# The second mixer's input projection in seven-product units entered by token halves, its results kept in DRAM, and squares of second halves added on GpSimd

## The chip, the cores and the metric

The kernel runs on one core of a Trainium2 chip. The metric is device time in microseconds of one launch, as the median of several runs. The profile shows one execution on that core. Engines are named as the profile names them: PE is TensorE (PEld its weight loads), DVE is VectorE, ACT is ScalarE, POOL is GpSimd, SP is SyncE, which here only issues DMAs.

## The reference

Two layers over 1024 tokens of width 1024, float32. Layer 0 has a mixer of gated blocks and forgetting attention, layer 1 a mixer of pooling and short convolution; after each come cross-attention into 256 memory tokens and a SwiGLU feed-forward of width 2816.

```python
for layer in range(2):
    h = rms_norm(x, g_mix[layer])
    y = even_mixer(h, ...) if layer % 2 == 0 else odd_mixer(h, ...)
    x = x + y
    x = x + memory_cross_attention(rms_norm(x, g_xa[layer]), rms_norm(mem, g_mem[layer]), ...)
    h = rms_norm(x, g_ffn[layer])
    x = x + (silu(h @ w_gate[layer]) * (h @ w_up[layer])) @ w_down[layer]

def odd_mixer(h, w_in, w_pool, s_pool, conv_w, w_out):     # w_in: 1024 x 2048
    z = h @ w_in
    zc, hd, gb, gc = z[:, :512], z[:, 512:1024], z[:, 1024:1536], z[:, 1536:]
    # pooling: 4 groups of 128, trailing mean over 2, 4, 8, 16 tokens minus the token,
    # then a 128 x 128 map per group and a scale per channel
    y_c = multiscale_pool(zc, w_pool, s_pool)
    # convolution: three taps over tokens on gc * hd, gated by gb
    y_d = short_gated_conv(hd, gb, gc, conv_w)
    return concat(y_c, y_d) @ w_out                          # w_out: 1024 x 1024
```

## The kernel before

**Number format.** Every float32 operand of a product is split in two: a high part, rounded by an ACT cast, and a low part, the remainder, from a DVE subtraction (`low`, line 551). A product of two such operands takes three matmuls: high x high, high x low, low x high. Data is held transposed: channels on the 128 partitions, tokens along the free dimension. A matmul is 128x128 by 128x512.

**Memory.** Two arenas in SBUF are handed out by a planner in Python as the program is built: `arena_r` (`self.R`, 35840 columns, for the split operands) and `arena_f` (`self.F`, 16384 columns, for plain float32). Each has a region "a" and a region "b". PSUM has eight banks of 512 columns.

**Order.** The program is a list of tasks (`self.add`), each with the operands that it needs. `run` walks the list. Before each task it prepares operands ahead, in order of first use: at most `la` columns ahead, at most `parts_max` columns of weight parts, and at most `raws` raw weights loaded and not yet consumed (`fetch_ahead`); an operand whose task has come must be made at once. `defer` puts off a step by a number of tasks. Each engine executes its instructions in the order in which they were emitted.

**Dense products.** `dense` (used by the second mixer) runs over row blocks of 128 and both halves of 512 tokens, three matmuls each. The normalised input h is not scaled by the token's norm; results are multiplied afterwards by `rbc`, the norm spread over all partitions.

**Seven-product units.** The feed-forward's projections use `Unit` and `seven`: two row blocks and two column blocks of the weight, and the two token halves, form 2x2 blocks, whose product is made with seven block products in place of eight (`Unit.make` forms the weight sums, lines 247 to 256; `Pair.make` those of a pair of input row blocks, lines 330 to 350). A unit over n pairs takes 7 x n x 3 matmuls. `collected` sums PSUM into two tiles of 128x1024 (lines 1973 to 1983) and hands on each quarter as it is finished; `onto_x` (line 2004) adds into x. In the gate and up projections POOL multiplies each gate quarter (line 2026) and makes sums of the products to be stored (line 2058).

**Entry into the feed-forward.** `cross` finishes x by token halves, first all row blocks of half 0, then of half 1. For each, `x_final` writes the half to DRAM (`xs`), scales half 0 in place and sums the squares: for half 0 on POOL (line 1909), for half 1 with four one-column matmuls per row block. `half_stats` then forms the tokens' norms; it and `spread`, which makes `rbc`, come after the first two products of the gate and of the up unit.

**Down projection.** The products of gate and up are stored in DRAM (`pq`) as the seven operands of each of 11 pairs. `VISITS` lists visits (column pair mp, first pair, last pair): each is one unit over some pairs, and a pair's operands stay in `arena_r` from its first to its last visit. The weights are loaded by POOL's queue. The last visits finish x.

**Second mixer.** At the end of the first feed-forward `chunk_sq` sums squares over whole rows (ACT, POOL lines 802 and 803) and `chunk_h` makes h and its low part for whole rows (lines 790, 791) in region "a" of `arena_r`, once `open_now` has taken it. `odd` then makes 16 blocks of z (`z_of`), each scaled by `rbc` (line 2213): four pooled groups (`pool_means`, lines 2225 to 2234; `pool_map`, lines 2250 and 2251) and twelve for the convolution (lines 2261 to 2273). x stays in `arena_f`, the split results in `arena_r`. The output projection comes in two halves (`out_half`, sums at line 1645): pooled results after the first two convolution blocks, convolution results at the end.

## Time and profile before

| | |
|---|---|
| median of 3 runs | 2389.23 us (2389.03 to 2389.98) |
| profiled execution | 2389.92 us, span 2388.1 us |
| mean granted TensorE clock | 0.994 |
| busy PE / DVE / ACT / POOL | 98% / 71% / 43% / 31% |
| first feed-forward, gate and up | from about 660 to 1080 us |
| its down projection | to about 1325 us |
| second mixer | about 1329 to 1595 us |
| second cross-attention, feed-forward | to the end |

In the profile a group's row gives the line, engine, operation, tiles with shapes, and count, then busy time and mean duration in ns, then the engine's idle time just before these instructions and what ended it. A line of the timeline gives start, length (us), engine, line, operation and how many were merged; brackets hold the idle time before. A line that belongs to a helper (551, 256, 539) serves many callers.

### The profile page before, as it was taken

The page shows a single profiled execution, that of the slowest core. Times are in us where ns is not written, and L with a number is a line of the kernel's source. Part 1 is how long each engine was busy: PE and PEld are TensorE (multiplying, and loading weights), DVE is VectorE, ACT ScalarE, POOL GpSimd, SP SyncE. Part 2 cuts the span into 40 slices and gives each one's busy share as a digit, 9 for nine tenths or more (in the row PEclk, how much of TensorE's full clock was granted, in tenths as well). Part 3 has the DMA queues.
Part 4 walks back from the last instruction along what each step waited for, and adds up shares of the span by engine and source line. Part 5 has one row for each costly group of instructions (what it writes and reads, how often), then busy time and mean ns, then how long its engine had stood idle before and what let it go on. Part 6 is the DMA issues. An engine that isn't in the chain of part 4 may idle for free. (4 is left out here: it accounts for less than half of the span.)

```text
span 2388.1 us, 31149 instructions
## 1 busy us (share of the span) xinstructions
PE 2337.4 (98%) x11358; PEld 1976.5 (83%) x11358; DVE 1705.6 (71%) x2505; ACT 1024.2 (43%) x1866; POOL 743.0 (31%) x745
## 2 busy tenths in 40 slices
PE   7999999999999999999999899999999999999999
PEld 7999879988888878887888788888877887877887
DVE  5456457864898888978677553356879988887666
ACT  6346356755554444445224221146544444444221
POOL 6542333343333343433011310033333334342000
PEclk9999999999999999999999999999999999999999
DMA  7336325431224444438873121021233444357783
GB/s 235 119 133 214 97 81 151 125 124 45 89 70 160 142 149 139 153 131 295 279 267 117 50 65 44 28 79 45 89 101 138 150 141 168 118 194 260 254 289 92
DMA packets 227074, 335.57 MB, mean 141 GB/s; under 512 B 12864, under 2 KB 128664, under 8 KB 226920
## 3 DMA queue, kind: packets, MB, share of 16 engines
q1 hardware_dynamic: 214544, 289.32, 37.1%
q0 software_dynamic: 12192, 44.21, 5.2%
q8 instruction: 89, 1.46, 0.3%
q14 instruction: 65, 0.53, 0.1%
q10 hardware_dynamic: 184, 0.05, 0.0%
HBM read 226.44 MB, written 107.09 MB: 140 GB/s over the span
## 5 line engine op out<-in xcount | busy, mean ns | idle before, releaser
L539 PE MATMUL psum_t<-arena_r 128*128 128x512 f32 (+4 forms) x10304 | 2255.4, 378 | 34.2 <-DVE arena_r L551 10.7
L539 PEld LDWEIGHTS psum_t<-arena_r 128*128 128x128 f32 (+1 forms) x10304 | 1856.2, 189 | 380.1 <-DVE arena_r L551 18.3
L551 DVE TENSOR_TENSOR arena_r<-arena_f,arena_r 128x512 fp32r<-128x512 f32 (+4 forms) x803 | 672.1, 857 | 167.5 <-PE psum_t L539 53.2
L256 ACT CAST arena_r<-arena_f 128x512 fp32r<-128x512 f32 (+2 forms) x504 | 282.4, 584 | 429.4 <-PE psum_t L539 252.6
L2026 POOL TENSOR_TENSOR arena_f<-arena_f 128x512 f32<-128x512 f32 x88 | 164.4, 1874 | 462.4 <-ACT arena_f L2025 462.3
L247 DVE TENSOR_TENSOR arena_f<-arena_f 128x512 f32<-128x512 f32 (+2 forms) x288 | 205.5, 717 | 81.4 <-DMA arena_f<-w_down 48.5
L1973 DVE TENSOR_TENSOR arena_f<-psum_t,arena_f 128x512 f32<-128x512 f32 x208 | 141.7, 685 | 51.6 <-PE psum_t L539 36.0
L2062 ACT CAST arena_r<-arena_f 128x512 fp32r<-128x512 f32 x140 | 86.8, 621 | 160.0 <-DVE arena_f L2033 58.2
L2058 POOL TENSOR_TENSOR arena_f<-arena_f 128x512 f32<-128x512 f32 x80 | 132.0, 1669 | 37.1 <-DVE arena_f L2033 35.6
L2004 DVE TENSOR_TENSOR arena_f<-psum_t,arena_f 128x512 f32<-128x512 f32 x160 | 106.4, 686 | 36.0 <-PE psum_t L539 35.7
L688 ACT CAST arena_r<-arena_f 128x1024 fp32r<-128x1024 f32 (+1 forms) x57 | 59.0, 1042 | 128.9 <-PE psum_t L539 90.3
L803 POOL TENSOR_TENSOR arena_f<-arena_f 128x1024 f32<-128x1024 f32 x21 | 60.6, 2884 | 127.8 <-ACT arena_f L802 61.9
L551 DVE TENSOR_TENSOR arena_r<-psum_t,arena_r 128x512 fp32r<-128x512 f32 (+3 forms) x124 | 84.6, 703 | 18.7 <-ACT arena_r L1443 6.8
L2025 ACT ACTIVATE arena_f<-arena_f 128x512 f32<-128x512 f32 x88 | 55.6, 632 | 81.6 <-DVE arena_f L2024 81.6
L236 POOL DMA_DIRECT2D arena_f<-w_down x38 | 30.3, 799 | 191.7 <-DVE arena_r L551 107.1
L1430 POOL TENSOR_SCALAR arena_f<-arena_f,small 128x640 f32<-128x640 f32 (+6 forms) x64 | 49.5, 781 | 108.8 <-DVE small L1429 104.7
L2033 DVE TENSOR_TENSOR arena_f<-arena_f 128x512 f32<-128x512 f32 x88 | 76.4, 868 | 4.5 <-POOL arena_f L2026 0.5
L2024 DVE TENSOR_TENSOR arena_f<-arena_f 128x512 f32<-128x512 f32 x88 | 66.2, 752 | 1.1 <-ACT arena_f L831 1.1
L562 POOL TENSOR_TENSOR small<-small,mhalf 128x4 f32<-128x4 f32 (+1 forms) x64 | 63.7, 995 | 5.2
L1425 ACT ACTIVATE arena_f<-psum_t,small 128x640 f32<-128x640 f32 (+6 forms) x64 | 47.5, 745 | 23.1 <-DVE small L1423 20.2
L2261 POOL TENSOR_TENSOR arena_f<-arena_f 128x1024 f32<-128x1024 f32 x4 | 10.4, 2598 | 139.5 <-DVE arena_f L2213 139.5
L1753 POOL TENSOR_SCALAR arena_f<-arena_f,small 128x256 f32<-128x256 f32 x64 | 33.3, 538 | 65.2 <-DVE small L1750 50.8
(192 smaller groups left out, 1533.9 us busy)
## 6 DMA issues: line engine op xcount, KB each, us to landing
pq<-arena_r SPq DMA_DIRECT2D x140, 512.0 KB
arena_r<-pq SPq DMA_DIRECT2D x280, 256.0 KB
arena_f<-w_gate SPq DMA_DIRECT2D x22, 1024.0 KB
arena_f<-w_up SPq DMA_DIRECT2D x22, 1024.0 KB
arena_r<-qk SPq DMA_DIRECT2D x48, 256.0 KB
qk<-arena_r POOLq DMA_DIRECT2D x16, 512.0 KB, 4.1
arena_f<-xa_wkv SPq DMA_DIRECT2D x16, 512.0 KB
arena_f<-xs SPq DMA_DIRECT2D x16, 512.0 KB
```

The lines of the kernel that those rows point to most:

```text
L247: getattr(T.nc, self.adds).tensor_tensor(out=out, in0=a, in1=b, op=what)
L256: T.nc.scalar.copy(out=hv, in_=src)
L539: self.nc.tensor.matmul(out=out, lhsT=lhsT, rhs=rhs, start=start, stop=stop, skip_group_check=again)
L551: getattr(self.nc, eng).tensor_tensor(out=out, in0=src, in1=high, op=ALU.subtract)
L562: self.nc.gpsimd.tensor_tensor(out=out, in0=in_, in1=self.mhalf[:, 0:in_.shape[-1]], op=ALU.pow)
L1973: nc.vector.tensor_tensor(out=o, in0=bank[q].ap, in1=o if other is None else other, op=ALU.add)
L2004: nc.vector.tensor_tensor(out=o, in0=bank[q].ap, in1=o, op=ALU.add)
L2024: nc.vector.tensor_tensor(out=q, in0=q, in1=r, op=ALU.mult)
L2026: nc.gpsimd.tensor_tensor(out=q, in0=q, in1=r, op=ALU.mult)
L2033: nc.vector.tensor_tensor(out=c[j].ap[:, o], in0=c[j].ap[:, o], in1=s.ap[:, o], op=ALU.mult)
L2058: nc.gpsimd.tensor_tensor(out=out, in0=a, in1=b, op=ALU.subtract)
L2062: nc.scalar.copy(out=t.ap[:, 0:512], in_=src)
```

## The change

The input projection of the second mixer is made of eight seven-product units (256 columns, four pairs) on the pair operands of x, entered as the feed-forwards are: the first feed-forward's last four visits call `x_final` for each finished quarter, with `mix` gains. For this the first feed-forward has a visit list of its own, in which the last four visits each hold pairs 8 to 10. Each quarter of z is scaled by `rbc`; pooling and convolution follow, deferred by a task. The eight results are written to DRAM in float32 (`ys`) by SP, read back (`Kept`, which is not fetched before it is there) and split; x is read back from `xs`. Both output halves come at the end. The squares of half 1 are summed on POOL like those of half 0, and `half_stats` takes eight sums; this holds for all three entries. Planner settings change in both down projections (`raws` 2 and then 1, and `parts_max`, `la` and `f_reserve` at the end), a pair is only begun when `arena_f` has room for it, and `cross` holds its probabilities in two buffers instead of one.

```diff
+VISITS_0 = ((1, 0, 1), (2, 0, 1), (3, 0, 2), (0, 0, 3), (1, 2, 4), (2, 2, 5), (3, 3, 5), (0, 4, 7), (1, 5, 7), (2, 6, 7),
+            (3, 6, 7), (0, 8, 10), (1, 8, 10), (2, 8, 10), (3, 8, 10))
...
+class Kept(Weight):
+    there = False
+    def ready(self):
+        return self.there
+    def fetch(self, T, must):
+        return self.there and T.load(self, must)
...
-        if not self.ready(2) and not must:
+        if not must and (not self.ready(2) or sum(map(T.F.room, "ab")) < 2 * 512 + 1024):
...
     def x_final(self, pairs, gname, layer, m, half):
...
         if half:
             pr.hi[e] = True
-            if m == 0:
-                self.sums = self.B.get()
-            sq = self.F.get(512, "ba")
-            nc.scalar.activation(out=sq.ap, in_=x, func=AF.Square)
-            def sums():
-                for b in range(4):
-                    self.mm(self.sums.ap[:, m * 4 + b:m * 4 + b + 1], sq.ap[:, b * P:(b + 1) * P],
-                            self.ones[:, 0:1], True, True)
-                sq.free()
-            self.defer(sums)
-            return
...
             def more():
-                nc.gpsimd.tensor_tensor(out=self.ssq.ap, in0=self.ssq.ap, in1=sq.ap, op=ALU.add)
+                nc.gpsimd.tensor_tensor(out=self.sqs[half].ap, in0=self.sqs[half].ap, in1=sq.ap, op=ALU.add)
                 sq.free()
             self.defer(more)
...
     def half_stats(self):
-        for b in range(4):
-            self.mm(ps.ap[:, 32 + b:33 + b], self.ssq.ap[:, b * P:(b + 1) * P], self.ones[:, 0:1], True, True)
+        for b in range(NB):
+            sq = self.sqs[b // 4].ap[:, b % 4 * P:(b % 4 + 1) * P]
+            self.mm(ps.ap[:, b:b + 1], sq, self.ones[:, 0:1], True, True)
...
         def down_end():
-            self.la, self.reserve, self.age = 3072, 0, 0
+            self.reserve, self.age, self.raws = 0, 0, 2
+            self.la, self.f_reserve, self.parts_max = 16384, 2048, 3072
...
             if n == 3:
-                self.add(lambda: setattr(self, "age", 0))
+                self.add(lambda: setattr(self, "raws", 2))
...
+            if left == 3:
+                self.add(lambda: setattr(self, "raws", 1))
...
-    def odd(self):
+    def odd(self, pairs):
...
+        def keep_y(k, t):
+            def fn():
+                nc.sync.dma_start(out=self.ys[k * P:(k + 1) * P, :], in_=t.ap)
+                t.free()
+                ys[k].there = True
+            self.defer(fn)
...
+        def quarter(kind, n, wait=0):
+            def fn(j, half, c):
+                o = slice(half * 512, (half + 1) * 512)
+                def scaled():
+                    q = c[j].ap[:, o]
+                    nc.vector.tensor_tensor(out=q, in0=q, in1=self.rbc.ap[:, o], op=ALU.mult)
+                if wait and (j, half) == (0, 0):
+                    self.defer(scaled, wait)
+                else:
+                    scaled()
+                if (j, half) in ((1, 0), (0, 1)):
+                    self.defer(lambda: post(kind, 2 * n + j, c[j]))
+            return fn
...
+        def tasks(kind, n, c0, wait=0, lead=()):
+            return self.seven(Unit(w_in, [(0, 4)], 4, c0 + n * 256, "ba", "ab"), pairs,
+                              self.collected(quarter(kind, n, wait)), lead)
+        def steady():
+            self.reserve, self.la, self.raws, self.f_reserve = 3072, 2048, 2, 6144
+        lead = [p.ops[i] for p in pairs[:2] for i in (2, 3, 6, 4, 5)]
+        pa = tasks("p", 0, 0, 5, lead)
+        pb = tasks("p", 1, 0, 5)
+        self.tasks += pa[:2] + pb[:2]
+        self.add(lambda: (self.half_stats(), self.spread()))
+        self.tasks += pa[2:]
+        self.add(steady)
+        self.tasks += pb[2:6]
+        self.add(lambda: pool_map(1), [wp])
+        self.tasks += pb[6:]
+        self.add(lambda: pool_map(0), [wp])
+        for n in range(2):
+            for kind, c0 in (("h", 512), ("c", 1536), ("b", 1024)):
+                ts = tasks(kind, n, c0)
...
+        def y_in(k):
+            def load(ap):
+                nc.sync.dma_start(out=ap, in_=self.ys[k * P:(k + 1) * P, :])
+            return Kept(S, load)
...
+        def out_start():
+            self.rbc.free()
+            self.reserve, self.la, self.f_reserve = 0, 4096, 0
+            self.x = [None] * KD
+            x_in(0)
+            x_in(1)
+        self.add(out_start)
...
+        for part in range(2):
+            if part:
+                self.add(mid)
+            for mp in range(4):
+                w = self.w_block(w_out, part * 512, 4, mp * 256, 256)
...
+                self.add(fn, ys[4 * part:4 * part + 4] + [w])
...
-        self.ffn(0, pairs[0], lambda m: self.chunk_h("mix", 1, m), self.open_h)
-        self.odd()
+        self.ffn(0, pairs[0], lambda m, half: self.x_final(pairs[2], "mix", 1, m, half), VISITS_0)
+        self.odd(pairs[2])
```

More of the change, by code (lines that the diff above doesn't have):

```diff
@@ L1765, in probs @@
             pt.free()
-            t = st["t"][n] = self.R.get(2048, "ba")
-            nc.scalar.copy(out=t.ap[:, 0:1024], in_=ps.ap)
+            th, tl = st["t"][n] = [self.R.get(1024, "ba") for _ in range(2)]
+            nc.scalar.copy(out=th.ap, in_=ps.ap)
             def rest():
-                self.low(t.ap[:, 1024:2048], ps.ap, t.f[:, 0:1024])
+                self.low(tl.ap, ps.ap, th.f)
                 ps.free()
@@ L1785, in mix @@
                 self.mm(ps.ap, vl, th, False, mb == 1)
-            t.free()
+            for x in t:
+                x.free()
             if half == 1:
@@ L1816, in project @@
             if pr == 1:
-                self.x_final(pairs, layer, m, halves[0])
+                self.x_final(pairs, "ffn", layer, m, halves[0])
         def free_o(pr):
@@ L2012, in onto_x, with ffn @@
         return after
-    def ffn(self, layer, pairs, finish=None, opening=None, emit=None):
+    def ffn(self, layer, pairs, finish, visits):
         nc, a = self.nc, self.a
@@ L2182, in ffn @@
                     rows.append((j * 256, 1))
-            u = Unit(wd, rows, hi - lo + 1, mp * 256, "ba" if n < 2 else "b", "b" if finish and left <= 4 else "ba", queue="gpsimd")
+            u = Unit(wd, rows, hi - lo + 1, mp * 256, "ba" if n < 2 else "b", "ba", queue="gpsimd")
             if n == 1:
@@ L2283, in odd @@
-        after = None
-        for g in range(4):
-            w = self.w_block(w_in, 0, KD, g * P, P)
-            self.add(lambda w=w: zt(w), [w])
-            if g == 0:
-                self.add(lambda: (self.stats(), self.spread()))
-            if g > 1:
-                self.add(lambda g=g: pool_map(g - 2), [wp])
-            self.add(lambda g=g: pool_means(g))
-        def conv(j, c):
-            w = self.w_block(w_in, 0, KD, 512 + c * 512 + j * P, P)
-            self.add(lambda w=w: zt(w), [w])
@@ L2297, in odd @@
[L2297 to L2317 removed]
+            keep_y(4 + j, t)
```

189 lines of the change are left out of this document (78 added, 111 removed).

## The prediction

> **What bounds the kernel now.** I read the page's busy shares first, then busy time in stretches of 20 us, then TensorE's timeline where those fell short, then the groups by shape.
>
> ```profile
> span 2388.1 us, 31149 instructions
> PE 2337.4 (98%) x11358; PEld 1976.5 (83%) x11358; DVE 1705.6 (71%) x2505; ACT 1024.2 (43%) x1866; POOL 743.0 (31%) x745
> ...
> 640.00:760.00 120.00, 118.92 (x542) 98.38 (x541) 105.76 (x139) 64.44 (x112) 44.58 (x30) 0.97 0.33 114
> 760.00:1060.00 300.00, 297.39 (x1304) 243.91 (x1304) 262.20 (x347) 135.99 (x241) 114.76 (x63) 1.00 0.41 143
> 1080.00:1318.00 238.00, 237.32 (x1042) 195.21 (x1042) 180.72 (x290) 81.50 (x144) 39.69 (x36) 1.00 0.70 236
> 1300.00:1320.00 20.00, 18.79 (x80) 14.37 (x78) 20.00 (x26) 9.45 (x11) 4.75 (x2) 1.00 0.48 138
> 1320.00:1340.00 20.00, 14.64 (x55) 11.63 (x56) 12.32 (x8) 4.30 (x5) 9.77 (x3) 0.83 0.07 21
> 1329.00:1409.00 80.00, 79.15 (x343) 64.64 (x344) 43.07 (x37) 18.09 (x26) 22.09 (x33) 0.97 0.18 53
> 1450.00:1558.00 108.00, 108.00 (x479) 89.41 (x478) 38.22 (x32) 16.10 (x15) 7.16 (x3) 1.00 0.13 40
> ```
>
> Columns of a stretch: length, busy us of PE, weight loads, DVE, ACT, POOL, granted clock, DMA share, GB/s. TensorE is busy 98%, so a matmul removed is time gained unless another engine then falls behind. The second mixer (from 1329) is plain TensorE work: in 1450:1558 PE has no gap and DVE is busy 35%. The feed-forward (760:1060), built of the seven-product units that the mixer is now to get, keeps DVE at 87%. The one real hole is where the first feed-forward ends and the mixer begins (1300 to 1340), with DVE at 20.00 of 20.00 just before it.
>
> **The change part by part.** Sums go against the profiled execution's 2389.92 us (span 2388.1 plus 1.8 around it); the median of the runs is 0.7 lower.
>
> *Matmuls.* Before, the input projection is 16 blocks x 8 row blocks x 3 terms x 2 halves = 768 matmuls of 512 columns. After, it is 8 units x 7 products x 4 pairs x 3 = 672. 96 go.
>
> ```profile
> 1449.63 50.71 PE L539 MATMUL psum_t<-arena_r 128*128 128x512 f32 x223
> ```
>
> 50.71/223 = 0.227 us each: **-21.8**. The pooled map (24) and the output projection (384) keep theirs. The visits still hold 44 pairs, so the down projection keeps its matmuls too.
>
> *Entry to the mixer.* The old whole-row conversions (8 of ACT, 8 of DVE, 128x1024) give way to 28 operands made as row pairs finish.
>
> ```profile
> 1301.88 17.32 PE L539 MATMUL psum_t<-arena_r 128*128 128x512 f32 x73 [0.39 <-DVE arena_r L551]
> 1320.07 3.71 PE L539 MATMUL psum_t<-arena_r 128*128 128x512 f32 x15 [0.87 <-DVE arena_r L791]
> 1329.07 12.45 PE L539 MATMUL psum_t<-arena_r 128*128 128x512 f32 x45 [5.29 <-DVE arena_r L791]
> ...
> 1369.25 10.96 PE L539 MATMUL psum_t<-arena_r 128*128 128x512 f32 x47 [0.78 <-ACT arena_r L557]
> ...
> 1722.44 8.01 PE L539 MATMUL psum_t<-arena_r 128*128 128x512 f32 x27
> ...
> 1748.41 1.98 PE L539 MATMUL psum_t<-arena_f,ones 128*128 128x512 f32 x4 [1.79 <-DVE arena_f L824]
> ...
> 1792.22 7.99 PE L539 MATMUL psum_t<-arena_r 128*128 128x512 f32 x34 [1.23 <-DVE arena_r L551]
> ```
>
> Loss now: gaps 0.39+0.87+5.29+0.78 = 7.3, and stretched rows (17.32, 3.71 and 12.45 against 73, 15 and 45 times 0.227) 3.3; together 10.6. The new entry is the one used before the second feed-forward; there the gaps 1.79+1.23 and 8.01 against 27 x 0.227 (1.9) make 4.9. Same code, so I take 4.9: **-5.7**. Ends: -10.6 (no loss) and +29 (the rival "entry stall").
>
> *Sums of squares.* At both feed-forward entries, half_stats drops from 36 one-column matmuls to 8 (32 of 36 summed the second halves). Each leaves two records.
>
> ```profile
> 666.10 0.95 PE L539 MATMUL psum_t<-ones,arena_f 128*128 128x1 f32 x8
> ...
> L1909 POOL TENSOR_TENSOR arena_f<-arena_f 128x512 f32<-128x512 f32 x14 | 19.3, 1376 | 40.8 <-ACT arena_f L1906 40.0
> ```
>
> 2 x 28 x 2 records x 0.95/8 = 13.3 us of TensorE time. In exchange POOL does 14 more adds of 1.376 us, 9.6 us per entry; POOL is busy 44.58 of 120 there, so they fit, and the sums, which now wait for POOL's last add with spread and the later products behind them on TensorE, have 48 matmuls (10.9 us) ahead of them. But DVE is busy 105.76 of 120 there and sets part of the pace, so I count half: **-6.7**. Ends: 0 and -13.3. At the mixer's entry 14 half adds replace 7 whole ones on POOL, and 8 sums stay 8: nothing.
>
> *DVE in the mixer.* A unit costs DVE 7 low parts, 4 weight sums, 4 sums out of PSUM and 4 scalings, all 128x512. Before, two blocks cost two low parts and two scalings of 128x1024.
>
> ```profile
> L551 DVE TENSOR_TENSOR arena_r<-arena_f,arena_r 128x512 fp32r<-128x512 f32 x604 | 498.0, 845 | 63.6 <-ACT arena_r L256 30.4 <-ACT arena_r L2062 12.0 <-PE psum_t L539 8.3
> L247 DVE TENSOR_TENSOR arena_f<-arena_f 128x512 f32<-128x512 f32 x224 | 171.3, 766 | 56.7 <-DMA arena_f<-w_down 23.9 <-DMA arena_f<-w_gate 23.9 <-DMA arena_f<-w_up 6.0
> L1973 DVE TENSOR_TENSOR arena_f<-psum_t,arena_f 128x512 f32<-128x512 f32 x208 | 141.7, 685 | 51.6 <-PE psum_t L539 36.0 <-ACT arena_f L1983 15.4
> L2024 DVE TENSOR_TENSOR arena_f<-arena_f 128x512 f32<-128x512 f32 x88 | 66.2, 752 | 1.1 <-ACT arena_f L831 1.1
> L551 DVE TENSOR_TENSOR arena_r<-arena_f,arena_r 128x1024 fp32r<-128x1024 f32 x75 | 101.8, 1361 | 82.6 <-PE psum_t L539 44.0 <-issue 22.1 <-ACT arena_r L688 7.6
> L2234 DVE SCALAR_TENSOR_TENSOR arena_f<-arena_f 128x1024 f32<-128x1024 f32 x4 | 4.9, 1226 | 5.6 <-POOL arena_f L2232 5.6
> L333 DVE SCALAR_TENSOR_TENSOR arena_f<-arena_f,gc 128x512 f32<-128x512 f32 x8 | 9.3, 1168 | 0.0
> ```
>
> A unit: 7 x 0.845 + 4 x 0.766 + 4 x 0.685 + 4 x 0.752 = 14.7 us, under 84 x 0.227 = 19.1 on TensorE. Eight units: 118. Beside them stand 22 pooling and convolution steps of 1.226 (27), 8 low parts of 1.361 (pooled maps and the first four stored results, 11), and about half the pair operands (14 x 0.845 + 8 x 1.168 = 21): 177 us against 696 x 0.227 = 158. At those means DVE is 19 us too slow. But those means come from stretches in which POOL is busy 38% (114.76 of 300) and reads the same memory; in the mixer it is 28% now (22.09 of 80). At the 0.685 of the group that reads PSUM the units take 104, the operands 15, the whole 157, and it just fits. Ends 0 and +19; nearest to the second row, with bursts (the eight pooling steps of the second unit fall together): **+4**. ACT (casts and copies) and the pooled maps' places among products cost nothing: ACT is busy 18.09 of 80 and 16.10 of 108 there.
>
> *Results through DRAM.* SP's queue gains 8 stores and 8 loads of results, 8 loads of x, 16 half-row stores of x, and has 8 weight loads fewer. The 16.8 MB over some 250 us add 67 GB/s to stretches that move 40 to 53 at a DMA share of 0.13 to 0.18: the volume is hidden. The order isn't. The store of result 6 waits for the last product of the last unit, and the first output weight (and under "raws" 2 the later results) are requested behind it on SP.
>
> ```profile
> arena_f<-xs POOLq DMA_DIRECT2D x16, 512.0 KB, 6.4
> ...
> L688 ACT CAST arena_r<-arena_f 128x1024 fp32r<-128x1024 f32 x56 | 58.4, 1050 | 128.9 <-PE psum_t L539 90.3 <-DMA arena_f<-o_w_out 24.5 <-DMA arena_f<-o_w_in 11.4
> ```
>
> Worst: sum 0.685 + scaling 0.752 + multiply 1.226, load 6.4, cast 1.05, low part 1.361 = 11.5 us of idle TensorE. None, if the weight is asked for earlier: 0. I take a third, as three of the four results are loaded by then: **+4**. The last four results have the first output half (192 x 0.227 = 44 us) as cover, x the whole queue: 0.
>
> *Visits of the first down projection.* One visit more means 8 more sums of 0.69 us on DVE, hidden (180.72 of 238). New is that visit (0, 8, 10) brings three stored pairs at once, where two was the most: 21 operands x 2 x 256 KB = 11.0 MB.
>
> ```profile
> 1240.00:1260.00 20.00, 20.00 (x90) 16.57 (x89) 13.97 (x25) 3.74 (x6) 1.60 (x2) 1.00 1.00 332
> ```
>
> At 332 GB/s they take 33 us; visit 11 and the two before it last 63+42+42 matmuls = 33 us, and the space comes free a visit earlier. **+1**, ends 0 and +13 (11.0 MB at the stage's mean 236 GB/s is 47 us). Fewer raw weights in flight (raws 2, then 1), parts_max 3072 in the second layer and halved probability buffers: 0, ends -2 and +2; parts still run several products ahead.
>
> Sum: -21.8 -5.7 -6.7 +4 +4 +1 = -25.2, so 2389.9 - 25.2 = 2364.7; as a median **2364**.
>
> **Rivals.**
> *DVE becomes the mixer's bound.* For it: 177 against 158 us above, and DVE at 87% in the same kind of unit. Against: in 760:1060 PE still does 297.39 of 300. Time: +19 for +4 and no gain at the entry: 2364 + 15 + 5.7 = 2385.
>
> *Entry stall (slower).* The down projection's last visits hold three pairs, 21504 of arena_r's 35840 columns, until the last visit releases them product by product. If the row pairs' operands (1024 columns each) find no room before, all 28 are made after it: 28 x 0.845 + 16 conversions of up to 1.168 = 42 us of DVE, with 48 matmuls (10.9 us) as cover before the product that needs them. Stall up to 29 in place of 4.9: 2364 + 24 + the lost clock behind a long gap (2.2 at 1329) + the output stall at its worst (7) = 2397. It is slower from about 23 of 28 left over; by columns, six parts of 768 beside the held pairs leave 9728, room for 9, so some 19 are left at the start of that visit and fewer at its end, which speaks against it.
>
> *The adds hold DVE.* POOL's adds could stop DVE instead of running beside it.
>
> ```profile
> 1326.24 6.07 DVE L791 SCALAR_TENSOR_TENSOR arena_r<-arena_f,gc,arena_r 128x1024 fp32r<-128x1024 f32 x2
> ...
> 1321.30 9.93 POOL L803 TENSOR_TENSOR arena_f<-arena_f 128x1024 f32<-128x1024 f32 x3 [4.17 <-ACT arena_f L802]
> ```
>
> Beside three POOL adds two DVE steps took 6.07 us, 3.0 each; the same kind took 1.226 to 1.361 above. If each of the 14 new adds holds DVE for its 1.376 us, that is 19 us on an engine at 88%, two thirds of which lands: the 6.7 are gone and some 5 more: 2364 + 6.7 + 5 = 2376. The Trainium skill (SBUF — State Buffer, section "SBUF: two separate sides") makes this a rule: DVE and GpSimd share one port pair as an exclusive lock, held for a whole instruction when both read two SBUF operands. By that rule the trace's 3.0 us are a wait, not slow arithmetic, and the trace agrees with it there.
>
> *Loads come late.* +13 for +1 in the down projection: 2376. For it: DMA share 1.00 in 1240:1260; against: PE had 20.00 of 20.00 in that same row.
>
> *All of it lands.* No stall anywhere, -10.6 and -13.3: 2389.9 - 21.8 - 10.6 - 13.3 = 2344.
>
> That the matmuls don't go is excluded: their number is in the loops.
>
> **How the numbers follow.** No change is within 0.2% (4.8 us), about what runs of this kernel can tell. Forecast (2352 to 2378) 0.55; adds hold DVE 0.08; loads late 0.06; all lands 0.09; DVE the bound (2378 to 2390) 0.14; entry stall 0.08. Faster: 0.55+0.08+0.06+0.09 and 0.04 of the 0.14 = 0.82. Same: 0.08 of the 0.14 and 0.01 of the last = 0.09. Slower: the rest, 0.09. The range 2346 to 2387 leaves out most of the entry stall, the half of "all lands" and a tip of the DVE case, about 0.17.
>
> **What would show it.** 672 matmuls in the mixer's input, its stretch about 22 us shorter; DVE at 85 to 95% there. At its entry gaps of 5 us in all instead of 7.3. One-column matmuls from 320 records to 208 at two per matmul. A gap before the first output product, released by a DMA of o_w_out or of the stored results: 4 us. Wrong would be: gaps released by DVE low parts all through the mixer; a gap over 10 us before its third product; gaps in the visit (0, 8, 10) released by DMA of stored pairs; the feed-forward's start no shorter than now.

## The result and the profile after

The changed kernel takes 2467.01 us (median of 4 runs, 2462.64 to 2470.92), the kernel before 2389.61 beside it (4 runs, 2389.03 to 2391.07): a ratio of 1.0323, 95% interval 1.0307 to 1.0338. It is slower by 77 us where 2364 was forecast. The profiled execution took 2462.64 us, with a span of 2460.6 against 2388.1 before.

The head of the profile's page after:

```profile
span 2460.6 us, 31139 instructions
PE 2338.4 (95%) x11150; PEld 1955.9 (79%) x11150; DVE 1790.8 (73%) x2668; ACT 1076.2 (44%) x1977; POOL 777.5 (32%) x775
```

TensorE has 208 instructions fewer and is busy for as long as before (2337.4 then). The groups of TensorE's work by shape tell why; the kernel before first (line 539), then the one after (line 554):

```profile
L539 PE MATMUL psum_t<-arena_r 128*128 128x512 f32 x8400 | 1960.0, 392 | 26.1 <-DVE arena_r L551 10.3 <-DVE arena_r L791 6.2 <-ACT arena_r L256 3.6
L539 PE MATMUL psum_t<-ones,arena_f 128*128 128x1 f32 x320 | 37.4, 242 | 0.0
```

```profile
L554 PE MATMUL psum_t<-arena_r 128*128 128x512 f32 x8304 | 1968.2, 395 | 93.1 <-DVE arena_r L566 24.4 <-ACT arena_r L270 24.1 <-ACT arena_r L360 12.1
L554 PE MATMUL psum_t<-ones,arena_f 128*128 128x1 f32 x208 | 27.7, 256 | 3.8 <-POOL arena_f L1913 3.8
```

Exactly the 96 wide matmuls and the 112 one-column records went that were forecast to go. But the 8304 wide ones that are left take 8.2 us more than 8400 did, and the idle time before them went from 26.1 to 93.1 us. So the removed work did leave TensorE; operands that came late took its place, twice: as gaps, and as slower matmuls (395 ns in the mean for 392, at a mean granted clock of 0.981 for 0.994).

Where it happened is read from windows that are cut where DVE begins the last result of a stage (for gate and up, the last multiplication of the two). First feed-forward (gate and up; down), mixer, and the second feed-forward's gate and up; before, then after. The columns are those of the prediction's first fence. Not shown are the second cross-attention (132.1 us before, 129.8 after) and the second down projection (217.2 and 210.7).

```profile
659.80:1106.40 446.60, 440.91 (x1937) 361.38 (x1938) 389.36 (x525) 205.33 (x366) 169.21 (x100) 0.99 0.43 150
1106.40:1325.60 219.20, 216.10 (x949) 177.47 (x947) 165.95 (x254) 72.65 (x119) 35.19 (x30) 1.00 0.64 216
1325.60:1593.30 267.70, 263.45 (x1156) 217.25 (x1157) 128.89 (x117) 60.08 (x66) 49.23 (x43) 0.99 0.17 50
1725.40:2170.90 445.50, 435.93 (x1906) 355.98 (x1906) 380.56 (x516) 200.15 (x359) 164.87 (x97) 1.00 0.44 151
```

```profile
662.90:1120.70 457.80, 440.87 (x1904) 359.03 (x1903) 398.58 (x533) 208.62 (x373) 178.85 (x102) 0.98 0.42 148
1120.70:1340.70 220.00, 211.81 (x920) 172.84 (x919) 173.81 (x286) 75.49 (x146) 44.54 (x42) 0.99 0.64 218
1340.70:1631.10 290.40, 258.79 (x1063) 205.79 (x1063) 192.12 (x242) 99.55 (x142) 65.28 (x49) 0.94 0.30 100
1760.90:2249.90 489.00, 450.00 (x1897) 357.32 (x1896) 394.39 (x536) 210.76 (x373) 159.84 (x103) 0.98 0.41 140
```

By the lengths of all six stages in order: +11.2, +0.8, +22.7, -2.3, **+43.5**, -6.5 us, and +3.1 before the first of them. The largest loss stands in the second feed-forward's gate and up projections, behind the mixer, where the prediction had counted a gain from fewer one-column sums and put the planner settings at nothing. The mixer is 22.7 longer instead of some 22 shorter, at a granted clock of 0.94.

Before, TensorE waited twice in the mixer, 5.3 and 0.8 us: the gaps at 1329 and 1369 that the prediction shows. After, what it waited for, grouped by line (in total, times, longest; the first four):

```profile
PE psum_t L554 <- ACT arena_r L703: 9.9, 2, 5.2
PE psum_t L554 <- ACT arena_r L360: 6.5, 1, 6.5
PE psum_t L554 <- ACT arena_r L572: 5.0, 3, 2.8
PE psum_t L554 <- ACT arena_r L270: 5.0, 4, 3.1
```

Four places: the output weights and results (703), the pair casts at the entry (360), the split of the pooled maps (572), and the weight casts (270). They are ACT casts, on an engine that is busy 34% there (99.55 of 290.4): ACT isn't full, its casts had to wait for what others owed them.

### The profile page after: what moved, and what is told of

The parts are those of the page before. It is cut to its first block, busy times and chain, and to the rows that moved or that the text cites. A ratio compares the mean times of both kernels' runs of the same rounds, so it can differ in the third digit from the quotient of the medians.

```text
span 2460.6 us, 31139 instructions
## 1 busy us (share of the span) xinstructions
PE 2338.4 (95%) x11150; PEld 1955.9 (79%) x11150; DVE 1790.8 (73%) x2668; ACT 1076.2 (44%) x1977; POOL 777.5 (32%) x775
## 5 line engine op out<-in xcount | busy, mean ns | idle before, releaser
L554 PE MATMUL psum_t<-arena_r 128*128 128x512 f32 (+5 forms) x10208 | 2263.3, 381 | 101.3 <-DVE arena_r L566 24.4
L566 DVE TENSOR_TENSOR arena_r<-arena_f,arena_r 128x512 fp32r<-128x512 f32 (+4 forms) x878 | 718.9, 841 | 142.5 <-ACT arena_r L270 51.3
L270 ACT CAST arena_r<-arena_f 128x512 fp32r<-128x512 f32 (+2 forms) x567 | 317.9, 582 | 487.6 <-PE psum_t L554 283.4
L261 DVE TENSOR_TENSOR arena_f<-arena_f 128x512 f32<-128x512 f32 (+2 forms) x324 | 233.5, 725 | 107.8 <-DMA arena_f<-w_down 59.3
L2029 POOL TENSOR_TENSOR arena_f<-arena_f 128x512 f32<-128x512 f32 x88 | 156.6, 1784 | 439.6 <-ACT arena_f L2028 431.9
L1976 DVE TENSOR_TENSOR arena_f<-psum_t,arena_f 128x512 f32<-128x512 f32 x240 | 163.2, 684 | 78.7 <-PE psum_t L554 39.4
L2061 POOL TENSOR_TENSOR arena_f<-arena_f 128x512 f32<-128x512 f32 x80 | 131.6, 1664 | 96.3 <-DVE arena_f L2036 94.7
L2065 ACT CAST arena_r<-arena_f 128x512 fp32r<-128x512 f32 x140 | 86.5, 620 | 136.9 <-DVE arena_f L2036 53.2
L2007 DVE TENSOR_TENSOR arena_f<-psum_t,arena_f 128x512 f32<-128x512 f32 x168 | 110.9, 684 | 28.2 <-PE psum_t L554 27.5
L1913 POOL TENSOR_TENSOR arena_f<-arena_f 128x512 f32<-128x512 f32 x42 | 61.4, 1465 | 75.6 <-ACT arena_f L1910 74.2
L818 POOL TENSOR_TENSOR arena_f<-arena_f 128x1024 f32<-128x1024 f32 x14 | 38.4, 2744 | 126.1 <-ACT arena_f L817 121.4
L2036 DVE TENSOR_TENSOR arena_f<-arena_f 128x512 f32<-128x512 f32 x88 | 64.3, 731 | 6.8 <-POOL arena_f L2029 3.0
L2027 DVE TENSOR_TENSOR arena_f<-arena_f 128x512 f32<-128x512 f32 x88 | 66.6, 756 | 0.3 <-ACT arena_f L846 0.2
L360 ACT CAST arena_r<-arena_f 128x512 fp32r<-128x512 f32 x72 | 43.6, 616 | 48.3 <-POOL arena_f L353 16.2
L1986 ACT COPY arena_f<-psum_t 128x512 f32<-128x512 f32 x60 | 35.0, 583 | 51.0 <-PE psum_t L554 44.6
```

The source lines that it names most:

```text
L261: getattr(T.nc, self.adds).tensor_tensor(out=out, in0=a, in1=b, op=what)
L270: T.nc.scalar.copy(out=hv, in_=src)
L554: self.nc.tensor.matmul(out=out, lhsT=lhsT, rhs=rhs, start=start, stop=stop, skip_group_check=again)
L566: getattr(self.nc, eng).tensor_tensor(out=out, in0=src, in1=high, op=ALU.subtract)
L1976: nc.vector.tensor_tensor(out=o, in0=bank[q].ap, in1=o if other is None else other, op=ALU.add)
L2007: nc.vector.tensor_tensor(out=o, in0=bank[q].ap, in1=o, op=ALU.add)
```

## The experiments

All were run once with a profile, beside a run of the kernel before (2387.7 to 2395.0 us in all), except "mended", which was run four times. Runs of the changed kernel itself lie 8 us apart, and the one whose trace is read is the shortest of its four: against their median every gain over it would be 4.4 us larger. Differences of single runs below some 5 us are not read, except where a stage shows them. Stage lengths are taken as above. Edits are shown in short form.

**Squares on POOL alone**, put into the kernel before:

```diff
-        sums of half 1's squares by one-column matmuls (x_final, half_stats)
+        self.sqs[half] += sq on gpsimd;  half_stats: 8 sums
```

> The kernel before, with one part of the change: the squares of second halves are added on POOL and half_stats takes 8 sums. Theory S (the added squares, not TensorE's sums, hold up both feed-forward entries, since POOL's adds stop DVE): first gate-and-up stage 447 -> about 458 us, second 446 -> about 457, time about 2410. Rival P (the first entry loses by the squares, the second by other things as well): second 446 -> 457 too, so this run alone can't separate them, but a second stage near 489 would say that the squares cause all of it (time 2443). Rival 0, the prediction's own step: 6.7 us faster, 2383.

**The changed kernel with half 1's squares on matmuls again**:

```diff
-        self.sqs[half] += sq on gpsimd, half 1
+        self.mm(self.sums.ap[:, m * 4 + b:...], sq.ap[...], self.ones[:, 0:1], True, True)
```

> The changed kernel with the squares of second halves summed on TensorE again, at all three entries. Theory S: first gate-and-up stage back from 458 to 447, the second from 489 to about 478, the mixer's entry a few us shorter; time about 2440. If the squares cause all of the second stage's loss: 2410. If the entries' loss has another cause (room in the arenas): within 5 us of 2467, or slower by the TensorE time of the sums.

The first took 2400.28 us, 10.2 more than the kernel before beside it; the second 2449.57, a span 12.8 shorter than the changed kernel's. So this part of the change costs some 10 to 13 us instead of gaining 6.7. The two don't find it in the same stages. In the first, the feed-forwards lose 1.9 and 6.9 us, and 4.6 are lost just ahead of the first. In the second, the first feed-forward gets back 6.1 (gate and up 444.9 for 457.8, down 226.8 for 220.0), and the mixer, at whose entry half 1's squares are on matmuls too, 11.1 (279.3); the prediction had put nothing at that entry. The second feed-forward's gate and up gets nothing back (490.4). Windows of 20 us at the first feed-forward's entry, of before, of after, and of the run with the matmuls back:

```profile
660.00:680.00 20.00, 20.00 (x109) 17.31 (x109) 19.83 (x23) 10.70 (x20) 9.37 (x6) 0.91 0.24 79
680.00:700.00 20.00, 20.00 (x82) 15.77 (x82) 15.90 (x24) 10.07 (x17) 6.67 (x4) 0.91 0.02 3
```

```profile
660.00:680.00 20.00, 16.36 (x70) 13.26 (x70) 19.96 (x21) 8.81 (x16) 12.14 (x9) 0.88 0.19 64
680.00:700.00 20.00, 15.00 (x46) 9.82 (x45) 18.57 (x22) 9.32 (x15) 10.42 (x6) 0.78 0.08 29
```

```profile
660.00:680.00 20.00, 19.58 (x114) 16.79 (x114) 19.83 (x25) 11.82 (x21) 8.82 (x6) 1.00 0.28 93
680.00:700.00 20.00, 20.00 (x87) 15.84 (x87) 16.22 (x23) 10.89 (x18) 7.26 (x5) 0.91 0.00 1
```

Before, TensorE had no gap here; with the adds on POOL it is busy 31.4 of 40 us and gets through 116 records instead of 191 (45 of the missing ones are one-column sums). One gap shows how. From the timeline after: two low parts of DVE, which take 0.68 us each when alone, take 3.44 beside POOL's adds (line 1913).

```profile
669.00 3.41 POOL L1913 TENSOR_TENSOR arena_f<-arena_f 128x512 f32<-128x512 f32 x2
671.19 3.44 DVE L566 TENSOR_TENSOR arena_r<-arena_f,arena_r 128x512 fp32r<-128x512 f32 x2
672.60 1.49 POOL L1913 TENSOR_TENSOR arena_f<-arena_f 128x512 f32<-128x512 f32 x1 [0.18 <-ACT arena_f L1910]
676.00 0.79 PE L554 MATMUL psum_t<-arena_r 128*128 128x512 f32 x1 [3.53 <-ACT arena_r L360]
```

The cast that ends TensorE's gap of 3.53 us waited for DVE's line 348, which begins at 674.56, as the two low parts end. No add of squares runs beside the later gaps up to 700; that they are lateness carried on is argued, not shown. POOL's last add is itself a link: it releases the 3.8 us before the one-column sums in the table by shape.

In the first feed-forward part of the gate and up's 11 us comes back in the down projection (squares alone: 458.0 and 209.7 us against 446.6 and 219.2), so stage by stage the two must be read together; the sum over the span is what counts.

**Planner settings.** Two runs put settings back behind the mixer: both of them, then `parts_max` alone.

```diff
         def mid():
             self.open_h()
-            self.la = 3072
+            self.la, self.parts_max = 3072, 4608     # and raws = 3 at the end of layer 1's cross in settings_back
```

> The changed kernel with parts_max set back to 4608 at the second half of the mixer's output projection and raws set back to 3 at the end of the second cross-attention, as both stood before. Theory P (these settings, left low by the change, cost the second gate-and-up stage some 31 of its 43 us): that stage 489 -> about 458, time 2436. Rival (it is the squares, or the order that the scheduler finds): stage stays near 489, time 2467.

> As settings_back, but only parts_max back to 4608; raws stays at 2 through the second cross-attention. If parts_max is what costs the second gate-and-up stage its 33 us (nine weight parts made ahead at the entry instead of six): stage near 456, time 2432. If raws is (the first units' weights asked for 4 tasks ahead instead of 15 to 23): stage near 489, time 2467. Both in part: between.

Measured: 2432.30 and 2427.39 us. `parts_max` alone takes 35.0 us off the span, 33.4 of them in the second feed-forward's gate and up, whose window reads, in the run with `parts_max` back:

```profile
1758.70:2214.30 455.60, 440.77 (x1899) 359.03 (x1899) 391.80 (x524) 207.69 (x369) 177.87 (x104) 0.97 0.43 150
```

and TensorE's waits for weight casts in that stage, after and with `parts_max` back:

```profile
PE psum_t L554 <- ACT arena_r L270: 12.9, 11, 4.8
```

```profile
PE psum_t L554 <- ACT arena_r L270: 5.4, 2, 4.8
```

Eleven waits for a weight cast in place of two; all TensorE's gaps in the stage together are 39.0 us against 14.8. The limit of 3072 columns was set for the first down projection's end and stayed on: six weight casts of 512 columns (line 270) are made well ahead of the stage, nine with the limit back at 4608. But the loss is not at the entry. The stage's first 40 us, and another 40 from 80 us on, after and with `parts_max` back:

```profile
1760.90:1800.90 40.00, 33.66 (x126) 25.47 (x125) 37.88 (x47) 21.23 (x36) 20.88 (x13) 0.87 0.19 60
1840.90:1880.90 40.00, 35.99 (x153) 27.98 (x152) 30.84 (x44) 15.15 (x27) 11.56 (x8) 1.00 0.52 171
```

```profile
1758.70:1798.70 40.00, 31.53 (x114) 22.87 (x114) 38.69 (x43) 19.02 (x31) 22.61 (x14) 0.79 0.12 40
1838.70:1878.70 40.00, 40.00 (x178) 33.14 (x177) 34.55 (x46) 18.48 (x34) 15.33 (x9) 1.00 0.33 119
```

At the entry TensorE does no less with the low limit; behind it, it loses up to 4.5 us of 40 in nearly every stretch, to the stage's end. That the low limit costs this is shown by the run; how it does so in the steady part is not settled. `raws` costs nothing that these runs can tell.

**Look-ahead in the mixer, and the results' way through DRAM.**

```diff
-            self.reserve, self.la, self.raws, self.f_reserve = 3072, 2048, 2, 6144
+            self.reserve, self.la, self.raws, self.f_reserve = 3072, 4096, 3, 3072    # mixer_ahead
-                nc.sync.dma_start(out=self.ys[k * P:(k + 1) * P, :], in_=t.ap)
+                nc.gpsimd.dma_start(out=self.ys[k * P:(k + 1) * P, :], in_=t.ap)      # ys_by_pool
-                nc.sync.dma_start(out=ap, in_=self.ys[k * P:(k + 1) * P, :])
+                nc.gpsimd.dma_start(out=ap, in_=self.ys[k * P:(k + 1) * P, :])        # ys_both_by_pool, with all three
```

> The changed kernel with more prepared ahead in the mixer: la 4096 for 2048, raws 3 for 2, f_reserve 3072 for 6144; raws back to 2 at the second output half. Theory L (the mixer's stalls are weights and stored results asked for too late): mixer 290 -> about 268 us, time 2445. Rival D (DVE is the mixer's bound, as in the prediction's rival): mixer 285 to 292, time 2462 to 2470.

> settings_back with one edit: the eight results are stored to DRAM by POOL's DMA queue instead of SP's. Theory Q (the stores wait on SP for the last products, and the weights and results queued behind them come late; the prediction's output step, at more than its worst price): the two stretches at the start of the output projection that lose 15 us lose under 4, time 2432 - 11 = 2421. Rival (the loss is the store's and load's own latency, or raws 2): within 3 us of 2432.

> parts_back with the results stored and read back by POOL's DMA queue, and with mixer_ahead's settings (la 4096, raws 3, f_reserve 3072). Theory Q2 (SP is held by the read-back of the late results as well as by their store, and a third raw weight is needed; either alone moved the stall elsewhere): the two stretches that lose 15 us at the start of the output lose under 4, the mixer 288 -> about 274, time 2427 - 13 = 2414. Rival (the latency of store and load): mixer above 284.

What they are about is seen in the waits of SP's queue after, 1500 to 1560:

```profile
SPq L2187 <- DVE arena_f L2240: 18.3, 2, 17.5
SPq L712 <- DVE arena_r L566: 12.5, 6, 5.8
```

One store of a result held the queue for 17.5 us, with output weights (line 712) and read-backs behind it. More look-ahead alone took one of the two gaps for line 703 away (4.9 us stay), and gave its gain back later (2467.15): the mixer is 6.4 shorter, the second gate and up 11.9 longer. The stores alone on POOL's queue gained nothing (2434.10 against 2432.30 of settings_back): the read-back of a late result held SP in their place. Stores, read-backs and look-ahead together, over parts_back, gave 2421.37 us; the mixer went from 287.9 to 279.5. The stage is what shows the gain: over the whole time it is 6.0, and the kernel before took 4.4 less beside this run than beside parts_back. Of the 9.9 us of TensorE's waits for line 703, 5.1 stay.

**Is it DVE's load, the room, or the order of tasks?** Four rivals, the first two over settings_back, the others over parts_back:

```diff
-                    nc.vector.tensor_tensor(out=q, in0=q, in1=self.rbc.ap[:, o], op=ALU.mult)    # no_scaling
-        self.ffn(0, ..., VISITS_0)
+        self.ffn(0, ..., VISITS)                             # two_held; prepared first are the pairs finished first, 3 and 0
-        self.tasks += pa[:2] + pb[:2]
+        self.tasks += [pa[0], pb[0], pa[1], pb[1]]           # first_later
-        pool_map(1), pool_map(0) among the p units, 3 and 2 among the first h unit
+        pool_map(1), (0) among the first h unit, 3 and 2 among the first c unit     # maps_later
```

> settings_back without the 32 multiplications of the mixer's quarters by the norms on DVE (that part of the computation is left out): 22 us of DVE work less in the mixer. Theory D (DVE is the mixer's bound): the stage falls from 292 by 12 to 20 us, time 2412 to 2420. Theory L (waits for weights, stored results and the order on the queues): by less than 6, time above 2426.

> settings_back with the old visit list in the first down projection too (14 visits, the last two of them hold two stored pairs instead of three), and the first finished row pairs, 3 and 0, as the ones prepared first. Theory R (the pair operands for the mixer's entry find no room in arena_r until the last visit, the prediction's entry stall): 7168 columns more are free, the 25 us lost around the entry become about 14, time 2421. Rival (DVE is busy there in any case): within 4 us of 2432.

> parts_back with the first products of the mixer in the order a0, b0, a1, b1 instead of a0, a1, b0, b1: 12 more matmuls (2.7 us) before the first product that needs the second row block of the last pair. Theory V (the last visit finishes that block's first half only at its sixth product, and the chain sum, square, scale, cast, low part is longer than the 21 matmuls before a1): the gap before a1 shrinks by 2 to 3 us, time 2424.5. Rival R2 (DVE and POOL are simply behind at that place): the loss moves on, time within 1 us.

> parts_back with the four pooled maps moved behind products 3 and 6 of the first h unit and of the first c unit. Theory M (in TensorE's order the maps stand before their inputs are ready, and TensorE waits for the pooling chain on POOL and DVE): the 8.5 + 4.8 us lost in the pooling part become under 6, time 2419. Rival D2 (DVE's burst of pooling steps, wherever the maps stand): unchanged within 3 us.

Taking 32 DVE multiplications out left the mixer as long (290.0 against 291.8 us): the sum of DVE's work was not its bound there. The old visits shortened the first down projection (211.1 against 217.2) and lengthened the mixer by 2: the loss at the entry moved (one wait for the pair casts is 12.6 us there). The order of the first products did nothing (2426.53 against 2427.39). Pooled maps made later were to gain some 8 us and lost 20 (2447.31), and their trace shows how the running means hold TensorE. Timeline, 1388 to 1404 us:

```profile
1391.50 4.23 POOL L2206 TENSOR_SCALAR arena_f<-arena_f 128x1 f32<-128x1 f32 x15 [6.73 <-ACT arena_f L2199]
1397.02 0.19 ACT L2199 COPY arena_f<-arena_f 128x1 f32<-128x1 f32 x1 [5.60 <-DVE arena_f L2208]
1401.63 0.58 ACT L1978 COPY arena_f<-psum_t 128x512 f32<-128x512 f32 x1 [1.13 <-DVE arena_f L2200]
1402.27 2.08 PE L554 MATMUL psum_t<-arena_r 128*128 128x512 f32 x4 [9.62 <-ACT arena_f L1978]
```

A mean is a chain that passes ACT, POOL and DVE in turn (2199, 2200, 2206, 2208). ACT comes to a copy of 0.19 us, finds its input not there, and stands for 5.6 us; behind it in order waits the copy that empties a PSUM bank (1978), and TensorE stands for 9.62. The order is not all of it: the copy's own last wait, 1.13 us, is for DVE's sum at line 2200. That copy reads a bank and writes a buffer of `arena_f`, so what it can wait for there is the buffer, which the means still used.

**The means.** Six runs over ys_both_by_pool (2421.37 us). First the chain rearranged:

```diff
-                nc.scalar.copy(out=nxt.ap[:, 0:d], in_=cur.ap[:, 0:d])
+                eng.tensor_copy(out=nxt.ap[:, 0:d], in_=cur.ap[:, 0:d])                 # copies_by_adder
-            for i in range(w - 1): nc.gpsimd.tensor_scalar(one column)
+            nc.vector.scalar_tensor_tensor(out=cur.ap[:, 0:w - 1], ..., in1=self.inv[:, 0:w - 1], ...)   # edges_at_once
+                eng = nc.vector, with both edits above                                  # means_on_dve
```

> From ys_both_by_pool (2421.37 us): the small copies of the means' steps (L2199, 0.19 us each) go from ACT to the engine that makes the step's sum, DVE or POOL. Theory A, ACT is held: in order, ACT waits at these copies for DVE and POOL (9.0 us in 1380:1420) with the copies of products out of PSUM behind them, and TensorE waits 4.7 us for one: the pooling stretch gets 4 to 8 us shorter, 2414 to 2417 us. Rival B, the chain itself is late (POOL's one-column multiplications 3.4 us, then DVE, then ACT's cast): unchanged within 2 us, or longer since the copies add to POOL and DVE.

> From ys_both_by_pool (2421.37 us): the 26 one-column multiplications of the four running means (POOL, 7.3 us) become four on DVE, of 15 columns at most, by a table made at the start. Theory E, they are the late part of the chain (DVE waited 3.3 us for them, and ACT 5.9 us behind that): 2412 to 2417 us. Rival F, the rest of the chain (sums and copies that pass ACT, DVE and POOL in turn) is late as well: within 3 us of 2421.

> edges_at_once, and the whole chain of each mean on DVE: four sums of the first step (POOL 2.08 us, on DVE about 1.22) and ten small copies (ACT 0.19 us). DVE gets about 4 x 1.22 + 10 x 0.1 = 6 us more. Rival F, the passing between engines costs most of the 24 us: 2400 to 2410 us. If it is DVE's own share that counts (12.2 us of the means before this edit): slower than edges_at_once by 2 to 6 us.

2427.09, 2417.73 and 2420.89 us, the mixer 281.6, 284.1 and 284.8 against 279.5. No single link is the cause: taking ACT's copies out of the chain, taking POOL's small multiplications out, or putting all of the means on DVE left the mixer 2 to 5 us longer. So the passing between engines, which means_on_dve takes out, is not shown to be the cost either. TensorE's wait for a bank stays about as long in all of them (4.68 us in ys_both_by_pool), and with all means on DVE it has another end:

```profile
1405.64 0.59 ACT L1981 COPY arena_f<-psum_t 128x512 f32<-128x512 f32 x1 [4.58 <-DMA ys<-arena_f]
1406.27 2.07 PE L557 MATMUL psum_t<-arena_r 128*128 128x512 f32 x4 [5.06 <-ACT arena_f L1981]
```

The copy that empties the bank (1981 in that kernel) now waits for a result's store to DRAM: again for a buffer of `arena_f`. Then the means left out, and their room kept:

```diff
         def pool_means(g, z):
+            st["p", g] = z
+            return                                                        # no_means
+            (buffers taken with self.F.get(S, "ba") and freed unwritten)  # room_held, ahead of it
```

> From ys_both_by_pool (2421.37 us), with the running means' sums left out (a part of the computation: the projected input goes to the pooled maps as it is), four chains of up to 4 sums, 4 copies and 15 one-column multiplications. Theory A and rival B alike: the two stretches of 84 matmuls beside them lose most of their 10.0 us over the matmuls' own time, so 2411 to 2415 us. Rival C, the mixer's operands for the seven-product units are late by themselves: not above 3 us gained, 2418 to 2421 us.

> no_means (2396.03 us; the means are left out, a part of the computation), but each mean takes its buffers of 4 KB in arena_f as before and gives them back unwritten. Theory G, the room that the means hold moves the planner's loads and operands: the 24 us come back, 2412 to 2421 us with PE gaps at the pooled maps and in the convolution. Theory H, the work of the chain and what waits for it in order on ACT, DVE and POOL: 2394 to 2400 us.

2396.03 and 2401.39 us; the mixer 255.3 and 260.2 against 279.5. Two stretches of the mixer (pooled maps, and the convolution 30 us behind them), in ys_both_by_pool, no_means and room_held:

```profile
1380.00:1420.00 40.00, 33.34 (x135) 25.48 (x134) 30.73 (x38) 13.79 (x25) 13.31 (x28) 0.96 0.27 93
1440.00:1460.00 20.00, 15.42 (x59) 11.75 (x58) 15.26 (x18) 5.93 (x9) 5.12 (x2) 0.91 0.24 80
```

```profile
1380.00:1420.00 40.00, 39.96 (x177) 32.77 (x176) 27.44 (x41) 18.36 (x27) 2.23 (x4) 1.00 0.30 105
1440.00:1460.00 20.00, 20.00 (x90) 16.55 (x89) 19.86 (x27) 7.21 (x12) 2.20 (x3) 1.00 0.36 118
```

```profile
1380.00:1420.00 40.00, 39.96 (x176) 32.77 (x175) 29.30 (x43) 18.16 (x26) 2.23 (x4) 1.00 0.27 94
1440.00:1460.00 20.00, 20.00 (x90) 16.58 (x89) 19.93 (x25) 7.64 (x13) 3.60 (x2) 1.00 0.35 105
```

Without the means' work TensorE has no gap and full clock in both stretches, also with DVE at 19.93 of 20. So of 24 us at least 19 are the work of the means and what waits for it, in order or for a buffer that it still uses. The other 5 are not shown to be room. They stand at the entry, ahead of any mean, where one subtraction on POOL (line 353) took 1.28 us in no_means and 5.49 in room_held, and TensorE's wait for the pair casts behind it was 2.3 and 6.5 us. The last of the six looks at the entry:

```diff
-            nc.gpsimd.tensor_tensor(out=t1, in0=t2, in1=b11, op=ALU.subtract)
+            self.subs(nc).tensor_tensor(out=t1, in0=t2, in1=b11, op=ALU.subtract)    # nc.vector for the mixer's pairs; t2 likewise
```

> From ys_both_by_pool (2421.37 us): the two sums of each mixer pair that POOL makes (L351, L353: 8 in all, up to 5.5 us beside a busy DVE) go to DVE at 0.7 us each. Theory P, POOL's stretched sum holds ACT's cast in order and TensorE behind it (6.5 us at the entry): that wait goes and the entry gets 4 to 7 us shorter, 2414 to 2417 us. Rival D, DVE without pause is what is late: 8 x 0.7 = 5.6 us more of it there move the wait on, unchanged within 2 us or up to 4 us longer.

It took 2423.10 us, the mixer 279.5 as before: rival D. What it meant to mend is in the timeline after:

```profile
1341.26 5.48 POOL L353 TENSOR_TENSOR arena_f<-arena_f 128x512 f32<-128x512 f32 x1
1341.27 0.74 DVE L356 SCALAR_TENSOR_TENSOR arena_r<-arena_f,gc,arena_r 128x512 fp32r<-128x512 f32 x1
1343.73 1.89 DVE L566 TENSOR_TENSOR arena_r<-arena_f,arena_r 128x512 fp32r<-128x512 f32 x3
1346.78 0.62 ACT L360 CAST arena_r<-arena_f 128x512 fp32r<-128x512 f32 x1 [4.82 <-POOL arena_f L353]
1349.22 1.27 POOL L353 TENSOR_TENSOR arena_f<-arena_f 128x512 f32<-128x512 f32 x1
1352.28 1.22 PE L554 MATMUL psum_t<-arena_r 128*128 128x512 f32 x2 [6.48 <-ACT arena_r L360]
```

The same subtraction on POOL takes 5.48 us beside a DVE without pause (seven instructions from 1341.27 to 1345.62, the first and the last three shown) and 1.27 eight us later. With it on DVE, TensorE's longest gap is 5.7 us, released by the square adds on POOL. The entry's loss has several links of one length, and no edit here took it away.

**Several mends together**, over parts_back: ys_both_by_pool, maps_later, first_later, and the squares on matmuls.

> All of these together, with the squares of second halves on TensorE: 2427 - 17 (squares) - 13 (output) - 8 (maps) - 2 = 2387 if the losses add up, that is about the kernel before; what stays lost is then the mixer's entry, some 20 us. If they overlap: 2395 to 2410.

2407.62 us (median of 4 runs, 2407.48 to 2409.41) against 2389.21, a ratio of 1.0076, 95% interval 1.0059 to 1.0093. It was put together before maps_later's loss was known and carries it. No version here beats the kernel before.

## Why the prediction was wrong, by its own steps

From the changed kernel's span of 2460.6 us, by edits: `parts_max` -35.0 (to 2425.6), the results' queue and the look-ahead -6.0 (2419.6), the means left out -25.4 (2394.2, without work that the kernel before does; some 5 of it at the entry, see above). The squares, measured by themselves, are another 10 to 13 us, which was not run on top of these.

- *Planner settings, 0 (-2 to +2)*: the step that failed most, +35. The prediction names "parts_max 3072 in the second layer" and puts it at nothing, with "parts still run several products ahead" as its only reason and no row behind it. Six parts are still several, and yet the second gate and up lost 33.4 us by it, along its whole length behind the entry. How fewer parts cost that much in the steady part stays open.
- *Matmuls, -21.8*: the 96 went, to the record. The step is right as work. That it would be time rested on the mixer's having no gaps, which was a property of the old mixer: its means ran beside plain products, with DVE busy 43.07 of 80 us (1329 to 1409). Beside units DVE is busy 30.73 of 40 (in ys_both_by_pool), and the means and the units wait for one another. Without the means the mixer falls to 255.3 us, 12.4 under the 267.7 of before (which has them).
- *DVE in the mixer, +4 (0 to +19)*: forecast as a sum of busy time, and of the kind that doesn't decide here. DVE is busy 66% in the mixer (192.12 of 290.4), not 85 to 95%, and 32 multiplications fewer changed nothing. The cost, at least 19 us, is that of the means beside units; which of their waits it is, for engines in order, for buffers or for DVE's bursts, no run here separates. The rival "DVE becomes the mixer's bound" had the size; its mechanism, a full DVE, is not what the mixer shows. "ACT (casts and copies) and the pooled maps' places among products cost nothing" is the sentence that failed: the four groups of waits on casts make 26.4 us of the mixer's gaps, and moving the maps cost 20. ACT had been judged by its busy share. (The pooling steps of the second unit on DVE are seven, not eight.)
- *Entry, -5.7*: the gaps before the mixer's first two units are not smaller but larger. Before, the windows 1300 to 1340 hold 33.4 us of TensorE work; after, 1320 to 1360 hold 27.1:

```profile
1320.00:1340.00 20.00, 15.44 (x59) 11.62 (x58) 20.00 (x27) 10.96 (x20) 9.16 (x6) 0.91 0.11 40
1340.00:1360.00 20.00, 11.64 (x43) 9.40 (x42) 13.40 (x22) 8.60 (x16) 14.86 (x8) 0.69 0.12 39
```

  That is 102 records for 135. Over the 168 records of wide matmuls on either side of the mixer's first, time over 0.227 us each is 26.4 us after and 14.6 before. So the term was some +7 to +12 for -5.7. "Same code, so I take 4.9" failed: the same code came behind another stage, one that keeps DVE at 20.00 of 20.00 until the mixer begins. The rival "entry stall" named the place and came to 13 to 18 us over the forecast's term where it was priced at 24 (its own numbers, 42 less 10.9, make a stall of 31, not 29). Its reason, room in `arena_r`, isn't borne out: two_held freed room there and gained nothing at the entry. What sets the rest of the entry stays open.
- *Sums of squares, -6.7*: 9.7 us of TensorE's records went (37.4 to 27.7) where 13.3 had been counted, and the kernel lost some 10 to 13. The rival "adds hold DVE" had the mechanism of the gap shown above; priced at 12 us over the forecast's term, the whole came to 17 to 20, with POOL's own lateness in it. The Trainium skill (SBUF — State Buffer, section "SBUF: two separate sides") lets whichever starts first, a DVE instruction with two SBUF inputs or a GpSimd instruction that reads SBUF, hold the shared pair for the whole instruction, while the other blocks. The trace agrees that each is stretched beside the other, and in both directions: DVE's low parts at 1.72 us each (3.44 for two) beside POOL's adds, and POOL's subtraction at 5.48 beside DVE. That last figure goes beyond one instruction: POOL's ended 1.12 us after the seventh DVE instruction in a row. The prediction had priced DVE's side alone.
- *Results through DRAM, +4 (0 to 11.5)*: the mechanism was right, a store of a late result with the output weights behind it; the size was 9.9 us of gaps at line 703, inside the range. Moving both directions off the queue, with more look-ahead, gave 8.4 back in the mixer and 6.0 over the span.
- *Visits, +1 (0 to +13)*: the down projection is 0.8 longer, and no gap for loads of stored pairs showed. With the old visits it was 6 shorter and the mixer 2 longer, 2.7 less over the span, which single runs can't tell: the term was inside its range.
- *The range*: it was built of single mishaps around one likeliest sum. Four of them came together (settings, means, entry, squares). The settings and the squares came out beyond their own bounds, the means and the entry within or near them, and the sum of the bad ends lay far above 2387. Of its signs of being wrong, one showed: the feed-forwards' start was no shorter (+3.1 us before the first, and longer entries).

## What to carry to other kernels

A setting of a hand-written planner has a place where it is set and a stretch in which it stays on: price a change of it at every stage up to where it is set again, and not by "still several ahead". Before a removed matmul is counted as time, look for chains of small steps beside it and for the buffers that they hold: an ACT that is busy a third of the time still stopped TensorE when the copy that empties a PSUM bank stood behind steps of 0.19 us, or waited for a buffer. When work moves to POOL, price what DVE does beside it and what POOL does beside DVE, not only POOL's free time.

## What the hardware showed that was not expected

Short gaps come with slower matmuls. In 680 to 700 us after, TensorE's gaps add up to 5.0 us of 20, and its 46 records take 15.00 us, 0.326 each, at a granted clock of 0.78. In the mixer, 31.6 us of gaps come with a clock of 0.94, against 4.3 and 0.99 before. The Trainium skill (TensorE: Matmul & The Clock Gate, Part 1) gives half speed after an idle window of about 3.4 us. The longest gap in 680 to 700 is 2.95 us (one of 3.53 ends at 676), and the trace has lower clocks also where TensorE shows no gap: 0.91 in 660 to 680 before, with 20.00 of 20.00 busy among one-column sums.

POOL can be held through a run of DVE's instructions. The 15 one-column multiplications of a mean, after:

```profile
1395.39 8.02 POOL L2206 TENSOR_SCALAR arena_f<-arena_f 128x1 f32<-128x1 f32 x15 [5.53 <-ACT arena_f L2199]
```

Thirteen of the fifteen took 0.19 us each. The other two took 3.15 and 1.84: each ended 0.05 us after a run of DVE instructions without pause that read `arena_f` and `arena_r` alone: four to 1398.49, three to 1400.89. Behind the first run DVE went on with a sum that reads PSUM, and beside that one POOL's next multiplications took 0.19 again. The mean over the group, 0.53 us, is the price of no instruction in it.
